# The first FFN's opening down product by seven block products instead of eight

## The chip, the cores and the metric

The kernel runs on one core of a Trainium2 chip. The metric is the device time of one launch in microseconds (us), the median of the runs shown; lower is better. A profiled execution gives the trace, and its own time stands beside those runs.

## The reference, cut to what matters

The kernel computes two layers of an encoder trunk for 640 tokens (512 of a prompt and 8 times 16 of running streams), all in fp32. Each layer has a first FFN, a mixer (convolution and attention) and a second FFN. The change touches the first FFN of the first layer alone, whose definition is:

```python
def _swiglu(h, w_gu, w_down):
    gu = h @ w_gu
    g, u = jnp.split(gu, 2, axis=-1)
    return (jax.nn.silu(g) * u) @ w_down
...
xp = xp + 0.5 * _swiglu(_rmsnorm(xp, norm_ffn1[l]), w_ffn1_gu[l], w_ffn1_down[l])
```

The model width is 1024 (8 tiles of 128), the FFN width 2816 (22 tiles of 128).

## The kernel before, in words

**Operands.** Activations lie with channels on the 128 partitions and the 640 tokens along the free axis, in two halves of 320. Every fp32 operand is split into a high and a low part (`hi` by a cast on ScalarE, called ACT, and `lo = src - hi` on VectorE, called DVE), and a product is three passes on TensorE, called PE: hi by hi, hi by lo, lo by hi. So one 128x128 weight tile against one half of the tokens is 3 matmuls of 320 columns.

**Eight or seven block products.** A plain product multiplies all tiles. A product "by seven" takes a 2x2 block of weights (two rows of tiles, two columns of tiles) and the two token halves with a Strassen-like scheme: seven block products instead of eight, at the price of sums of weights (DVE), sums and differences of activations (DVE) and more intermediate results that are copied out of PSUM (ACT, DVE). The seven are named by their activation operand: X11, X21, XN6, XT5, XT7, X22, XT4. The gate and up products of a tile (`gate_up`, a "unit") are made by seven in every case but four: 84 matmuls a unit, in blocks of 12, in the order X11, X21, XN6, XT5, XT7, X22, XT4.

**The first FFN, "a0".** `FFNS` gives it chunks of 4, 4, 4, 4, 4 and 2 tiles and a plain opening of 4: the gate and up products of tiles 0 to 3 are eight plain products (`opening`, L604), since the operands of the scheme are made meanwhile. Tiles 4 to 21 are units (`gate_up`, L743). The down product of a chunk's tiles is spread over the units of the next chunk. `by_seven` (L78) says for which chunks it is made by seven, by `down_rows` (L936), in two calls of four output rows each (84 matmuls a call), after the second and third unit of the next chunk. For a down product by seven the activations of two neighbouring tiles form a `Pair` (L872): from the even tile's `E` and the odd tile's `O` come X11 and XT5, X21 and X22, and in `rest` XN6, XT7 and XT4; they are split into hi and lo too. In the kernel before, chunk 0 (the opening's tiles) is not by seven: its down product is 8 plain rows of 24 matmuls, two rows after each of the units 4, 5, 6 and 7.

**What sets the order.** The weights come as a stream of 512 KB pieces (`wst`), whose order follows from `ffn_order`; `load` fetches them, `source` makes the sums of weights, `prep` casts a slice (a "slab") of up to 128x1024 to hi, and `flush` queues the subtraction for lo. The hi and lo of slabs have three buffers each. Until unit 6 of this FFN PE, DVE and ACT run in the order in which the program is written (`ORDERED`, L206, and `free`, L1029); from unit 6 on only PE does, and the tile framework orders DVE and ACT. All three take their instructions in order.

Each unit ends with a `tail` (L854) that multiplies the gate by the up result and splits the product; it is put on the list `tails` and called later: in the kernel before at the start of the down rows behind the unit (L1063), in units without such rows ahead in the next unit behind its block X11 (L823), and in `down_rows`. The opening's own splits (`parts`, L688) are put on the same list: unit 4, the first, calls two behind X11 (L774) and the others behind X21 (L788).

In `gate_up` of a later unit the order around the list is:

```python
            mul(pa, s0, 0, X11, every, True, True)
            ACT.copy(c1, pa)
            prep(used[0] + 1)
            ...
            for t in tails:
                t()
            tails.clear()
            ...
            mul(pa, s1, 0, XN6, every, False, True)
            ACT.copy(u2, pa)
            ...
            mul(pa, s2, 0, XT7, every, False, True)
```

XN6, XT7 and XT4 add to one PSUM tile `pa`; what stands in it is copied out between them (`c1`, `u2`), and XT4 waits for DVE's `add(g[:, t2], pa, c5)` behind XT7.

Of the kernel before, what the change touches and what calls it, by code (L numbers as in the profile page):

```python
# [13 lines left out]
ALU = mybir.AluOpType  # L14
# [17 lines left out]
FT = FF // P  # L32
# [36 lines left out]
def chunk_at(name, j):  # L69

    at = 0
    for n in FFNS[name][0]:
        if j < at + n:
            return at, n
        at += n


def by_seven(name, j):  # L78

    at, n = chunk_at(name, j)  # L80
    return n == 4 and at >= FFNS[name][1] and at + n < FT


def ffn_order(name):
# [93 lines left out]
def halves(t):  # L178
    return t.rearrange("p (a b) -> p a b", a=2)
# [3 lines left out]
def trunk(ctx: ExitStack, tc: tile.TileContext, xin, wst, small, pbias, samplebias, kcache, vcache,  # L183
# [36 lines left out]
    def split(hi, lo, src):  # L220
        ACT.copy(hi, src)
        DVE.tensor_tensor(out=lo, in0=src, in1=hi.bitcast(F32), op=ALU.subtract)
# [5 lines left out]
    for kind, inside in kinds():  # L228
        n = len(fourth)
# [371 lines left out]
            ACT.activation(early, epst, AF.Silu)  # L601
            self.known = True

    def opening(fp, name, goff, n, put, tails):  # L604

        ACT.copy(early, epst)
        ex = Expand(fp, name, goff)
        h = []  # L610
        whi, wlo = (wp.tile([P, CH], F32R, tag=f"w{t}", name=f"w{t}0", bufs=3) for t in ("hi", "lo"))
        ready.append((whi, wlo))
        for k in range(KT):
            g = sm[:, goff + k : goff + k + 1]
            hi = hp.tile([P, T], F32R, tag="hhi", name=f"hhi{name}_{k}")
            lo = hp.tile([P, T], F32R, tag="hlo", name=f"hlo{name}_{k}")
            ACT.activation(hi, x[k], AF.Copy, scale=g)
            c = slice(k * P, (k + 2) * P)
            if k % 2 == 0:
                ACT.copy(whi[:, c], raws[0][:, c])  # L620
            DVE.scalar_tensor_tensor(out=lo, in0=x[k], scalar=g, in1=hi.bitcast(F32),
                                     op0=ALU.mult, op1=ALU.subtract)
            if k % 2 == 0:
                DVE.tensor_tensor(out=wlo[:, c], in0=raws[0][:, c], in1=whi[:, c].bitcast(F32),
                                  op=ALU.subtract)
            h.append((hi, lo))
        flush()

        made = {2: (0, 1), 3: (2, 3), 4: (4,), 5: (5, 6), 6: (7,)}
        us, gs, ps = [], [], []  # L630

        def out(i):

            j, up = divmod(i, 2)
            if not up:
                gs.append(tmp(f"g{name}_{j}"))
                if j:
                    scaled(gs[j], ps[i], ex.rho)
                    ACT.activation(gs[j], gs[j], AF.Silu)
                else:  # L640
                    ACT.copy(halves(gs[j]), two(ps[i]))
                return
            u = tmp(f"u{name}_{j}") if j > 1 else fp.tile([P, T], F32, tag="cap", name=f"u{name}_{j}", bufs=5)
            us.append(u)
            if j:
                scaled(u, ps[i], ex.rho)
                DVE.tensor_tensor(out=u, in0=u, in1=gs[j], op=ALU.mult)
            else:
                ACT.copy(halves(u), two(ps[i]))

        def begun():
            ex.total(att(f"nps{name}"))
            ex.root()
            ex.diagonal()

        at = {2: {4: begun}, 3: {1: lambda: ex.spread([att(f"nbc{name}_{a}")[:, :HT] for a in range(2)])}}
        for i in range(2 * n):
            ps.append(acc(f"po{name}_{i}"))
            product(ps[i], h, at.get(i, {}))
            if i > 1:  # L660
                out(i - 1)
            if i == 0:
                for k in range(KT):
                    ex.square(k)
                    ex.add()
                    if k == 1:
                        out(0)
                    if k == 4:
                        flush()
            if i == 1:  # L670
                continue
            if i == 3:
                g, u = gs[0], us[0]
                DVE.tensor_tensor(out=g, in0=g, in1=ex.rho, op=ALU.mult)
                ACT.activation(g, g, AF.Silu)
                DVE.tensor_tensor(out=u, in0=u, in1=ex.rho, op=ALU.mult)
            flush()
            for m in made.get(i, ()):
                ex.final(m, False)
            if i == 3:  # L680
                DVE.tensor_tensor(out=u, in0=u, in1=g, op=ALU.mult)
            if i == max(made):
                ex.rest()
        ahead()
        begin()
        out(2 * n - 1)

        def parts(j, u):  # L688
            hi = hp.tile([P, T], F32R, tag="hhi", name=f"ahi{name}_{j}")
            lo = hp.tile([P, T], F32R, tag="hlo", name=f"alo{name}_{j}")  # L690
            split(hi, lo, u)
            put(j, (hi, lo))


        for j in sorted(range(n), key=lambda j: j < 2):
            tails.append(lambda j=j: parts(j, us[j]))
        ex.rest = None
        return ex

# [40 lines left out]
        with soon():  # L740
            last(pa)

    def gate_up(fp, n, ex, first, tails, put, j, pair, later, at):  # L743

        pa, pb, pc = (att(f"p{i}{n}")[:, :HT] for i in "abc")

# [15 lines left out]
        if first:  # L762
# [24 lines left out]
            add(u[:, t1], pb, c1)  # L787
            for t in tails[2:]:  # L788
                t()
            tails.clear()  # L790
            s2 = quiet()
            prep(len(ready))
            flush()
# [78 lines left out]
    class Pair:  # L872
# [8 lines left out]
        def product(self, n, u, g, hi, lo):  # L881
            if self.E is None:

                z = self.E = self.fp.tile([P, 3, HT], F32, name=f"de{n}", tag="even", bufs=1)
                DVE.tensor_tensor(out=z[:, 0:3:2], in0=halves(u), in1=halves(g), op=ALU.mult)
                DVE.tensor_tensor(out=z[:, 1], in0=z[:, 0], in1=z[:, 2], op=ALU.subtract)
                at, kinds = slice(0, 2), (X11, XT5)
            else:

                z = self.O = self.fp.tile([P, 5, HT], F32, name=f"do{n}", tag="odd", bufs=1)  # L890
                DVE.tensor_tensor(out=z[:, 3:5], in0=halves(u), in1=halves(g), op=ALU.mult)
                at, kinds = slice(3, 5), (X21, X22)
                self.later.append(self)
                self.work = self.rest()
            flush()
            ACT.copy(halves(hi), z[:, at])
            self.low(halves(lo), halves(hi), z[:, at])
            self.keep(kinds, hi, lo)

        def low(self, lo, hi, z):  # L900
            DVE.tensor_tensor(out=lo, in0=z, in1=hi.bitcast(F32), op=ALU.subtract)
# [6 lines left out]
        def rest(self):  # L908
            E, O = self.E, self.O
            for o, a, b in ((XN6, E[:, 1], O[:, 4]), (XT4, O[:, XN6], O[:, 3])):  # L910
                DVE.scalar_tensor_tensor(out=O[:, o], in0=a, scalar=-1.0, in1=b,
                                         op0=ALU.mult, op1=ALU.subtract)
            DVE.tensor_tensor(out=O[:, XT7], in0=O[:, 4], in1=E[:, 2], op=ALU.subtract)
            yield
            hi, lo = (hp.tile([P, T], F32R, tag=f"h{i}", name=f"t{i}{self.name}") for i in ("hi", "lo"))
            ACT.copy(halves(hi), O[:, 1:3])
            yield
            self.low(halves(lo), halves(hi), O[:, 1:3])
            self.keep((XN6, XT7), hi, lo)
            yield  # L920
            hi, lo = (self.fp.tile([P, HT], F32R, tag=f"t4{i}{self.i}", name=f"t4{i}{self.name}", bufs=1)
                      for i in ("hi", "lo"))
            ACT.copy(hi, O[:, 0])
            yield
            self.low(lo, hi, O[:, 0])
            self.keep((XT4,), hi, lo)
            yield
# [90 lines left out]
    def ffn(name, fp, ex, goff, after, end=False):  # L1018
# [7 lines left out]
        hold[0] = True  # L1026

        mode = ExitStack()
        free = min(j for j in range(FT) if by_seven(name, j)) + 2  # L1029

        def order(engines):
            mode.close()
# [1 line left out]

        order(ORDERED)
        if plain:
            ex = opening(fp, name, goff, plain, act.__setitem__, tails)
        for what, a in ffn_order(name):
            if what == "gu" and a == free:
                order({mybir.EngineType.PE})  # L1040
# [4 lines left out]
            if what == "gu":  # L1045
                pair = None
                if by_seven(name, a):
                    i, odd = divmod(a - chunk_at(name, a)[0], 2)
                    if not odd:
                        at = chunk_at(name, a)[0]  # L1050
                        rows = at and by_seven(name, at - 1)
                        pairs[a] = Pair(fp, f"{name}_{a}", i, later, TURNS[i if rows else i + 2])
                    pair = pairs[a - odd]
                gate_up(fp, f"{name}_{a}", ex, a == plain, tails, act.__setitem__, a, pair, later,
                        a - chunk_at(name, a)[0])
                continue
            if what == "rows":
                ms, js = a
# [145 lines left out]
    class Operands:  # L1204
# [24 lines left out]
        def parts(self, hi, lo, z):  # L1229
            ACT.copy(hi, z)  # L1230
            DVE.tensor_tensor(out=lo, in0=z, in1=hi.bitcast(F32), op=ALU.subtract)
# [496 lines left out]
    fp = ExitStack()  # L1728
# [157 lines left out]
```

## Time and profile before

| | |
|---|---|
| median of 3 runs | 2522.48 us (2522.24 to 2522.82) |
| profiled execution | 2522.74 us, its span 2521.0 us |
| granted TensorE clock, mean | 0.999 |
| busy: PE, weight loads | 2502.0 us (99%), 2441.3 us (97%) |
| busy: DVE, ACT, POOL | 2117.7 us (84%), 1325.1 us (53%), 185.6 us (7%) |
| instructions | 42929, of them 17192 matmuls |

A row of the timeline gives start, duration, engine, line and operation, output and input tiles, shape, count and the idle time before it with what ended it. A duration is longer than the step from one instruction to the next on the same engine, since neighbours overlap. In the table of windows each row is a stretch of the span: its length, each engine's busy time with its number of instructions, the granted TensorE clock and the share of the DMA engines.

### The profile page before, as it was taken

The numbers are of one execution on the slowest core, as the hardware profiler recorded it, in microseconds if no ns is written. First come the engines' busy times: TensorE is split into PE (matmuls) and PEld (weight loads), VectorE is DVE, ScalarE is ACT, GpSimd is POOL, SyncE is SP. The second block draws the span as 40 slices with busy tenths as digits, with TensorE's granted clock in tenths as the row PEclk, the third lists the DMA queues.
The fourth block names the chain that finished last, engine by engine and source line by source line (L and its number), as shares of the span: only waits on it lengthen the run. The fifth ranks groups of instructions, "written<-read, shape, count | busy, mean of one in ns | idle before, by whom it ended". The sixth has DMA issues, their size and how long they took to land.

```text
span 2521.0 us, 42929 instructions
## 1 busy us (share of the span) xinstructions
PE 2502.0 (99%) x17192; PEld 2441.3 (97%) x17192; DVE 2117.7 (84%) x3347; ACT 1325.1 (53%) x2084; POOL 185.6 (7%) x249
## 2 busy tenths in 40 slices
PE   9999999999999999999999999999999999999998
PEld 9999999888999999999999999998889999999998
DVE  7889888878677899988699999888786768899997
ACT  7445556664444545555455555557644455455553
POOL 0000112111000001000001000021110000010000
PEclk9999999999999999999999999999999999999999
DMA  4233444334222234343224343443342222243434
GB/s 144 76 105 103 115 115 126 107 114 162 76 85 92 75 101 115 105 110 100 84 76 112 110 116 100 115 118 124 129 138 84 76 93 76 86 114 109 123 100 99
DMA packets 99320, 265.40 MB, mean 105 GB/s; under 512 B 9680, under 2 KB 45136, under 8 KB 99120
## 3 DMA queue, kind: packets, MB, share of 16 engines
q1 hardware_dynamic: 69408, 220.76, 26.7%
q0 software_dynamic: 28992, 41.26, 9.3%
q8 instruction: 135, 2.21, 0.4%
q10 hardware_dynamic: 720, 0.65, 0.1%
q14 instruction: 65, 0.53, 0.1%
HBM read 222.70 MB, written 7.94 MB: 91 GB/s over the span
## 4 chain that ended last, share of the span: by engine, by line
PE 92%; ACT 4%; DVE 3%; issue 1%; DMA 0%; DVEq 0%; ACTq 0%
PE pab L397 12%; PE paa L397 11%; PE pcb L397 6%; PE pca L397 6%; PE daa L952 5%; PE py L374 4%; PE po L374 4%; PE qa L397 4%; PE pdb L374 4%; PE dab L952 4%; PE pbb L397 3%; PE pba L397 3%; PE poa L374 2%; PE pda L374 2%; PE pv L1392 2%; PE ma_cv L397 2%
## 5 line engine op out<-in xcount | busy, mean ns | idle before, releaser
L312 DVE TENSOR_TENSOR wlo<-raw,whi 128x1024 fp32r<-128x1024 f32 (+1 forms) x566 | 585.6, 1037 | 177.8 <-ACT whi L307 172.6
L307 ACT CAST whi<-raw 128x1024 fp32r<-128x1024 f32 (+1 forms) x566 | 509.1, 903 | 366.6 <-PE pbb L397 38.6
L307 ACT CAST whi<-s 128x1024 fp32r<-128x1024 f32 (+1 forms) x152 | 144.4, 950 | 279.5 <-issue 89.3
L397 PE MATMUL pab<-xhib,whi 128*128 128x320 f32 x704 | 218.1, 310 | 0.3
L397 PE MATMUL pab<-xhib,wlo 128*128 128x320 f32 x704 | 217.3, 309 | 0.0
L397 PE MATMUL pab<-xlob,whi 128*128 128x320 f32 x704 | 217.2, 309 | 0.0
L397 PE MATMUL paa<-xhia,whi 128*128 128x320 f32 x640 | 198.0, 309 | 1.0 <-ACT c_a L833 0.6
L397 PE MATMUL paa<-xhia,wlo 128*128 128x320 f32 x640 | 197.5, 309 | 0.0
L397 PE MATMUL paa<-xloa,whi 128*128 128x320 f32 x640 | 197.5, 309 | 0.0
L312 DVE TENSOR_TENSOR wlo<-s,whi 128x1024 fp32r<-128x1024 f32 (+1 forms) x152 | 166.3, 1094 | 9.8 <-ACT whi L307 9.8
L397 PEld LDWEIGHTS pab<-xhib,whi 128*128 128x128 f32 x704 | 132.1, 188 | 0.9 <-ACT c_b L833 0.8
L397 PEld LDWEIGHTS pab<-xlob,whi 128*128 128x128 f32 x704 | 132.1, 188 | 0.2
L397 PEld LDWEIGHTS pab<-xhib,wlo 128*128 128x128 f32 x704 | 132.1, 188 | 0.0
L397 PEld LDWEIGHTS paa<-xhia,whi 128*128 128x128 f32 x640 | 120.1, 188 | 1.6 <-ACT c_a L833 0.9
L397 PEld LDWEIGHTS paa<-xloa,whi 128*128 128x128 f32 x640 | 120.1, 188 | 0.1
L397 PEld LDWEIGHTS paa<-xhia,wlo 128*128 128x128 f32 x640 | 120.1, 188 | 0.0
L976 POOL DMA_DIRECT2D x<-c_b x28 | 33.8, 1209 | 1105.6 <-ACT c_b L969 457.8
L397 PE MATMUL pcb<-xhib,wlo 128*128 128x320 f32 x352 | 108.8, 309 | 0.0
L397 PE MATMUL pcb<-xlob,whi 128*128 128x320 f32 x352 | 108.6, 309 | 0.0
L397 PE MATMUL pcb<-xhib,whi 128*128 128x320 f32 x352 | 108.6, 309 | 0.0
L976 POOL DMA_DIRECT2D x<-c_a x36 | 43.6, 1212 | 865.1 <-ACT whi L307 386.4
L251 DVE TENSOR_TENSOR raw<-raw,raw 128x512 f32<-128x512 f32 x152 | 103.7, 683 | 0.8
(681 smaller groups left out, 7943.2 us busy)
## 6 DMA issues: line engine op xcount, KB each, us to landing
raw<-in_wst SPq DMA_DIRECT2D x378, 512.0 KB, 3.5
x<-c_a POOLq DMA_DIRECT2D x36, 320.0 KB, 4.2
x<-c_b POOLq DMA_DIRECT2D x28, 320.0 KB, 4.1
kc<-in_kcache SPq DMA_DIRECT2D x32, 256.0 KB, 3.8
vc<-in_vcache SPq DMA_DIRECT2D x16, 512.0 KB, 4.7
x<-u_a POOLq DMA_DIRECT2D x18, 320.0 KB, 5.4
x<-u_b POOLq DMA_DIRECT2D x14, 320.0 KB, 5.5
bias<-in_pbias POOLq DMA_DIRECT2D x16, 256.0 KB, 3.6
```

The source lines that it names most:

```text
L251: DVE.tensor_tensor(out=out, in0=a, in1=b, op=ALU.add)
L307: ACT.copy(hi[:, d], src[:, c])
L312: DVE.tensor_tensor(out=lo, in0=src, in1=hi.bitcast(F32), op=ALU.subtract)
L374: PE.matmul(ps[:, a, :HT], w, x[:, a * HT : (a + 1) * HT], start=first and j == 0, stop=last and j == 2)
L397: PE.matmul(ps, a, b, start=start and kp == 0 and j == 0, stop=stop and kp == NP - 1 and j == 2, skip_group_check=True)
L952: PE.matmul(ps[u], w, y, start=start and i == 0 and j == 0, stop=i == 1 and j == 2, skip_group_check=True)
L976: POOL.dma_start(rows(r, cols), z, accum_op=ALU.add)
L1392: PE.matmul(pv[t], xx[:, t * P : (t + 1) * P], w[:, kk * AW : (kk + 1) * AW], start=c == 0 and kk == 0 and j == 0, stop=c == KT // 2 - 1 a ...
```

## The change

`by_seven` now holds for chunk 0 too, so the down product of tiles 0 to 3 is made by two calls of `down_rows`, after units 5 and 6, instead of 8 plain rows after units 4 to 7. The opening's activations become two `Pair`s (0 and 1, 2 and 3). Since the opening has already multiplied gate and up, `Pair.times` copies the product on ACT where there is no gate. Pair 2/3 is made in unit 4 (parts 2 and 3 behind X11, its `rest` in one piece behind X21). Pair 0/1 is kept for unit 5: the list `after` (parts 0 and 1 and their `rest`) becomes the list of tails at the end of unit 4's first half, unit 4's own tail is put behind it, and all four are called behind X11 of unit 5. Two more things follow. Unit 4 has no down rows behind it, so its tail moves into unit 5. And pair 4/5 takes its later steps at the places of `TURNS` for chunks that follow a chunk by seven. `free` stays 6.

```diff
 def by_seven(name, j):
 
     at, n = chunk_at(name, j)
-    return n == 4 and at >= FFNS[name][1] and at + n < FT
+    return n == 4 and at + n < FT
...
-        def parts(j, u):
+        def parts(j):
             hi = hp.tile([P, T], F32R, tag="hhi", name=f"ahi{name}_{j}")
             lo = hp.tile([P, T], F32R, tag="hlo", name=f"alo{name}_{j}")
-            split(hi, lo, u)
+            pairs[j - j % 2].product(f"{name}_{j}", us[j], None, hi, lo)
             put(j, (hi, lo))
 
-
-        for j in sorted(range(n), key=lambda j: j < 2):
-            tails.append(lambda j=j: parts(j, us[j]))
+        for i in range(n // 2):
+            pairs[2 * i] = Pair(fp, f"{name}_{2 * i}", i, later, ())
+
+        def rest(i):
+            for _ in pairs[2 * i].work:
+                pass
+
+        tails += [lambda: parts(2), lambda: parts(3), lambda: rest(1)]
+        after += [lambda: parts(0), lambda: parts(1), lambda: rest(0)]
         ex.rest = None
         return ex
...
             for t in tails[2:]:
                 t()
-            tails.clear()
+            tails[:] = after
             s2 = quiet()
...
                 z = self.E = self.fp.tile([P, 3, HT], F32, name=f"de{n}", tag="even", bufs=1)
-                DVE.tensor_tensor(out=z[:, 0:3:2], in0=halves(u), in1=halves(g), op=ALU.mult)
+                self.times(z[:, 0:3:2], u, g)
                 DVE.tensor_tensor(out=z[:, 1], in0=z[:, 0], in1=z[:, 2], op=ALU.subtract)
...
                 z = self.O = self.fp.tile([P, 5, HT], F32, name=f"do{n}", tag="odd", bufs=1)
-                DVE.tensor_tensor(out=z[:, 3:5], in0=halves(u), in1=halves(g), op=ALU.mult)
+                self.times(z[:, 3:5], u, g)
                 at, kinds = slice(3, 5), (X21, X22)
-                self.later.append(self)
+                if self.spots:
+                    self.later.append(self)
                 self.work = self.rest()
...
+        def times(self, out, u, g):
+            if g is None:
+                ACT.copy(out, halves(u))
+            else:
+                DVE.tensor_tensor(out=out, in0=halves(u), in1=halves(g), op=ALU.mult)
...
-        free = min(j for j in range(FT) if by_seven(name, j)) + 2
+        free = min(j for j in range(plain, FT) if by_seven(name, j)) + 2
```

The other lines of the diff hand the lists and the pairs through (`opening(..., tails, held, pairs, later)`, `gate_up(..., held if plain else ())`).

More of the change, by code (lines that the diff above doesn't have):

```diff
@@ L602, in spread, with opening @@
             self.known = True
-    def opening(fp, name, goff, n, put, tails):
+    def opening(fp, name, goff, n, put, tails, after, pairs, later):
         ACT.copy(early, epst)
@@ L741, in seven, with gate_up @@
             last(pa)
-    def gate_up(fp, n, ex, first, tails, put, j, pair, later, at):
+    def gate_up(fp, n, ex, first, tails, put, j, pair, later, at, after=()):
         pa, pb, pc = (att(f"p{i}{n}")[:, :HT] for i in "abc")
@@ L1036, in ffn @@
         if plain:
-            ex = opening(fp, name, goff, plain, act.__setitem__, tails)
+            held = []
+            ex = opening(fp, name, goff, plain, act.__setitem__, tails, held, pairs, later)
         for what, a in ffn_order(name):
@@ L1054, in ffn @@
                 gate_up(fp, f"{name}_{a}", ex, a == plain, tails, act.__setitem__, a, pair, later,
-                        a - chunk_at(name, a)[0])
+                        a - chunk_at(name, a)[0], held if plain else ())
                 continue
```

## The prediction

> **What bounds the kernel now.** I read the page first, then the windows of the units around the change, then the timelines of PE, DVE and ACT there.
>
> ```profile
> span 2521.0 us, 42929 instructions
> PE 2502.0 (99%) x17192; PEld 2441.3 (97%) x17192; DVE 2117.7 (84%) x3347; ACT 1325.1 (53%) x2084; POOL 185.6 (7%) x249
> ```
>
> PE is busy nearly all the time, so a matmul less is time won, but only where nothing else makes PE wait. DVE at 84% is the next engine.
>
> The windows that I cut at PE's first block of each unit (columns: length, then busy time and instructions of PE, weight loads, DVE, ACT, POOL, then clock and DMA share):
>
> ```profile
> 67.06:86.42 19.36, 19.36 (x134) 19.36 (x133) 17.19 (x25) 9.68 (x14) 0.00 (x0) 1.00 0.25 82
> 86.42:105.79 19.37, 19.37 (x135) 19.37 (x133) 15.19 (x23) 7.31 (x11) 0.00 (x0) 1.00 0.26 82
> ...
> 144.52:156.84 12.32, 12.32 (x86) 12.32 (x85) 9.83 (x17) 5.87 (x9) 0.00 (x0) 1.00 0.27 86
> 156.84:181.48 24.64, 24.64 (x170) 24.64 (x169) 23.45 (x37) 13.64 (x19) 2.96 (x3) 1.00 0.35 97
> 181.48:206.55 25.07, 24.95 (x171) 24.68 (x170) 20.72 (x30) 13.08 (x19) 3.40 (x4) 1.00 0.53 126
> ```
>
> Rows one and two are units 4 and 5, each with two plain down rows behind it; then unit 8 alone, unit 9 with a `down_rows`, unit 10 with the second one. A unit of 84 matmuls takes 12.32 us, so a matmul steps by 0.1467 us and a block of 12 by 1.76. 24.64 is exactly two units' worth: no wait. 25.07 is 0.43 more: the second `down_rows` of a chunk stalls PE a little. DVE is filled to 17.19 of 19.36 in unit 4 and its rows, and to 23.45 of 24.64 where a unit and rows by seven stand together.
>
> **Part one, the matmuls.** Eight plain rows are 8 x 24 = 192 matmuls, two `down_rows` are 168. 24 x 0.1467 = 3.5 us less. That is 0.14%, and about 0.2% (5 us) is what a measurement of this kernel can tell from no change: what decides is the cost on the other engines.
>
> **Part two, where the new work lies.** Units 4 and 5 and the first `down_rows` run DVE and ACT in program order. The prices are the steps from start to start, in unit 4's own rows (ACT first, then DVE):
>
> ```profile
> 68.36 1.06 ACT L307 CAST whi<-raw 128x1024 fp32r<-128x1024 f32 x1 [1.92 <-DVE raw L251]
> 69.31 0.42 ACT L767 COPY c_a<-paa 128x320 f32<-128x320 f32 x1
> 69.62 1.36 ACT L221 CAST ahia<-ua 128x640 fp32r<-128x640 f32 x2
> 70.88 0.43 ACT L777 COPY c_a<-pca 128x320 f32<-128x320 f32 x1
> 72.54 0.42 ACT L786 COPY c_a<-paa 128x320 f32<-128x320 f32 x1 [1.23 <-PE paa L397]
> ...
> 69.85 1.22 DVE L312 TENSOR_TENSOR wlo<-raw,whi 128x1024 fp32r<-128x1024 f32 x1
> ...
> 76.78 0.48 DVE L251 TENSOR_TENSOR ga<-paa,c_a 128x320 f32<-128x320 f32 x1
> ...
> 81.12 0.68 DVE L251 TENSOR_TENSOR s<-raw 128x512 f32<-128x512 f32 x1
> 81.84 0.69 DVE L251 TENSOR_TENSOR s<-s,raw 128x512 f32<-128x512 f32 x1
> 82.45 0.82 DVE L857 TENSOR_TENSOR ga<-ga,rhoa 128x640 f32<-128x640 f32 x1
> 83.30 0.82 DVE L885 TENSOR_TENSOR dea<-ua,ga 128x640 f32<-128x640 f32 x1
> 84.16 0.49 DVE L886 TENSOR_TENSOR dea<-dea 128x320 f32<-128x320 f32 x1
> 84.57 1.22 DVE L312 TENSOR_TENSOR wlo<-s,whi 128x1024 fp32r<-128x1024 f32 x1
> 85.70 0.82 DVE L901 TENSOR_TENSOR aloa<-dea,ahia 128x640 fp32r<-128x640 f32 x1
> 86.44 0.69 DVE L251 TENSOR_TENSOR raw<-raw,raw 128x512 f32<-128x512 f32 x1
> 87.04 0.69 DVE L251 TENSOR_TENSOR raw<-s,raw 128x512 f32<-128x512 f32 x1
> ```
>
> Steps on ACT: 0.96 (1024 wide), 0.63 (640), 0.32 (320); a 512 cast I take half-way, 0.53. On DVE: 1.14 (1024), 0.74 (640), 0.41 (320), 0.60 (512), and 0.12 more where an instruction reads the result of the one just before. A result can be read by another engine about 0.05 after its shown duration. With these I walk the three queues; the same walk of the order before puts unit 5's first block at 86.55, where the trace has 86.42.
>
> *Unit 4.* Unstalled, PE starts its blocks at 67.06, 68.82, 70.58, 72.34, XT7 at 74.10, 75.86, XT4 at 77.62. DVE starts at 69.85 with the slab's lo: 1.14, then pair 2's difference 0.41 (71.40). ACT casts it 71.53 to 72.26; DVE has idled 0.9; low part to 73.05. ACT copies and casts part 3 until 73.67, DVE idles 0.7, low part to 74.46. The copy of `u2` that XT7 needs stands behind these casts and ends at 74.32: XT7 0.3 late. Then DVE: 0.41 for u, the three sums of `rest` 1.36, 0.9 idle for their cast, low parts 0.74 + 0.41, the slab's lo 0.60, and only then the add to g that XT4 needs, done at 79.38. XT4 starts at 79.43 instead of 77.62: **1.8 us** of waiting in unit 4. Before, `rest` was not there, and the same add ran at 76.8.
>
> *Unit 5.* The down rows that stood between units 4 and 5 (48 x 0.1467 = 7.0 us in which DVE caught up) are gone, so unit 5 starts right behind and waits 0.3 for its first lo and 0.2 for its second. DVE is behind. From 79.3 it does 0.54 and 0.41 for unit 4's g and u, 1.14 for unit 5's first lo, 1.34 for the two weight sums of its second slab, 0.41 for g, idles 0.83 for the cast of that slab, then its lo 1.14 and the sums of slab three 1.20: 86.3. Now the four list items come, ahead of all of unit 5's own copies on both queues. ACT: the slab's cast 0.96, copy of part 0; DVE waits for it until 88.19. Then DVE: difference 0.41, the slab's lo 1.14, low 0.74, 0.44 waiting, low 0.74, three sums 1.36, 0.9 waiting, low 0.74 + 0.41, and tail 4: 0.74 + 0.87 + 0.54. That ends at 97.3. Only then can ACT cast tail 4's operand (0.63), and behind it in ACT's queue stands the copy of `u2`, done at 98.41. XT7 was ready at 88.76. **9.7 us** of waiting.
>
> This queue is in the trace already, in the other layer's first FFN, where one tail lies in the same place of its second unit (waits of PE, then ACT's timeline):
>
> ```profile
> PE paa L397 <- ACT c_a L833: 0.6, 1, 0.6
> ...
> 1285.14 0.73 ACT L896 CAST ahia<-dea 128x640 fp32r<-128x640 f32 x1 [0.50 <-DVE dea L886]
> 1285.77 0.42 ACT L833 COPY c_a<-paa 128x320 f32<-128x320 f32 x1
> ```
>
> L833 is the copy of `u2`, L896 the tail's cast that waits for DVE. One item just overruns the block; here there are four.
>
> *The first `down_rows` and unit 6.* Its operands are ready by then. Its evictions are 3.0 us on DVE (three 640, two 320) and some 2 on ACT, its weights three 1024 slabs and a 512, with four 512 sums. Together with tail 5 DVE stays 2 to 3 us behind PE, which costs PE little: 0.6 us until the second `down_rows` (lo of unit 6's second slab late). The second `down_rows` I give the 0.4 that it has elsewhere. Cover goes nowhere else: POOL is at 0.00 in the windows of units 4 and 5, so its six added accumulating transfers queue behind nothing, the weight bytes stay the same, and the DMA share of 0.53 in the last window is far from full.
>
> **Part three, the clock.** A PE that has been idle comes back slow. At the kernel's start matmul pairs step by 0.53, later by 0.29; at the end, where PE is nearly idle, the granted clock falls to half:
>
> ```profile
> 8.25 0.74 PE L374 MATMUL poa<-hloa,whi 128*128 128x320 f32 x2
> 8.78 0.74 PE L374 MATMUL poa<-hhia,wlo 128*128 128x320 f32 x2
> ...
> 12.36 0.46 PE L374 MATMUL poa<-hloa,whi 128*128 128x320 f32 x2
> 12.65 0.46 PE L374 MATMUL poa<-hhia,wlo 128*128 128x320 f32 x2
> ...
> 5.86:11.45 5.59, 5.59 (x21) 5.47 (x21) 5.12 (x9) 4.96 (x8) 0.00 (x0) 1.00 1.02 389
> ...
> 2506.00:2513.40 7.40, 6.06 (x49) 5.68 (x47) 5.40 (x13) 2.80 (x7) 0.00 (x0) 1.00 0.29 102
> 2513.50:2520.00 6.50, 1.22 (x2) 0.50 (x2) 4.49 (x11) 0.00 (x0) 0.00 (x0) 0.50 0.83 284
> ```
>
> The 21 matmuls of the first 5.59 us step by 0.267 instead of 0.147 (the clock column shows 1.00 there, since the record of the clock begins with a change; I go by the steps): 21 x 0.12 = **2.5 us**. A 9.7 us hole should bring this back once; shorter ones need not. Bounds: nothing (the clock holds) and twice that. The Trainium skill, "TensorE: Matmul & The Clock Gate", section "What's actually happening", says that the clock halves after an idle window of about 3.4 us and comes back after a busy one; the rows above agree, and by a 3.4 us warm-up it would cost about 1.5 instead of 2.5.
>
> **Sum.** -3.5 + 1.8 + 0.5 + 9.7 + 0.6 + 0.4 + 2.5 = **+12.0 us**. The profiled execution (2522.74, of which 1.74 lie outside its span) would become 2534.7; it stands 0.26 over the median, so the median goes from 2522.5 to **2534.5**. If DVE's idling in the walk vanished (some 7.3 us with the small waits), XT7 of unit 5 would come 12.0 - 7.3 = 4.7 late in all, the clock would hold, and the change would end near +1. If shown durations counted instead of steps, about 28 instructions of DVE cost 0.08 more each: +14.
>
> **Rivals.** (A) *The matmuls alone count.* PE is the fullest engine, and DVE at 84% and ACT at 53% absorb the rest: 3.5 less and 0.4 for the second rows, 2519.4, no change that a measurement tells. For it: PE never waits in the four units before, and by the windows a unit with rows by seven runs unstalled at 24.64. The Trainium skill, "Perfetto Trace Analysis", section "Identifying the Most-Contended Engine", says to improve the engine with the highest occupancy first; here PE. Against: those units are ordered by the framework, and no opening's pairs are made there. It decides if the copy of `u2` in unit 5 is not behind the casts. 3%. (B) *DVE and ACT overlap better*: the hole is 2 to 5 us, the clock holds, -3.5 + 1.8 + 3.5 + 1 = about +3, 2525.5: within the bound. 6%. (C) *The clock holds although the hole is as walked*: 2532.0. 13%. (D) *DVE does not catch up*: it gains 24.64 - 23.45 = 1.2 per unit and rows, and with 3 us behind at unit 6 it needs more than one such stretch; PE then waits about 3 more in units 6 to 8: 2537.5. 13%.
>
> **How the numbers follow.** The forecast has 64%. With C and D slower has 90%; A and B make 9% within 0.2%; nothing offers 5 us of gain, so 1% is left for faster. The range runs from a hole 4 us shorter without a slow clock, 2528, to D with a little more, 2538.5.
>
> **What would show it.** Right: PE's matmuls fall by 24; a wait of PE on ACT for the copy of `u2` near 8 to 11 us in one piece, about 20 us after unit 4's start; behind it some 20 matmuls at 0.27; a smaller wait of XT4 of unit 4 on DVE; DVE busy without gaps from 70 to about 120. Wrong: PE without waits between 67 and 141, or a copy of `u2` that runs ahead of the tail's cast.

## The result and the profile after

The changed kernel takes 2534.06 us (median of 6 runs, 2533.51 to 2534.72); the kernel before took 2522.82 us beside it (2522.24 to 2523.11). The ratio is 1.0045 with an interval of 1.0035 to 1.0056: 11.2 us slower. The profiled execution took 2533.69 us, with a span of 2531.6.

The head of the page after:

```profile
span 2531.6 us, 42953 instructions
PE 2500.7 (99%) x17168; PEld 2438.6 (96%) x17168; DVE 2131.2 (84%) x3373; ACT 1336.9 (53%) x2104; POOL 192.7 (8%) x255
```

The 24 matmuls are gone (17192 to 17168), DVE has 13.5 us more to do and ACT 11.8, and still the shares of PE, DVE and ACT are the same. From these shares alone one would not see a loss. The waits of PE after, longest first:

```profile
PE paa L397 <- ACT c_a L839: 10.2, 2, 9.6
PE poa L374 <- ACT whi L620: 5.7, 1, 5.7
PE paa L397 <- DVE ga L251: 1.3, 1, 1.3
```

The second row is the start of the kernel and was there before. The first is new, nearly all in one piece, and L839 is the copy of `u2`; the other 0.7 us of that row lies in the other layer's first FFN, where the kernel before waited 0.6, and the rows of this copy in the experiments hold it too. The third is unit 4's XT4 behind the add to g. PE's timeline around the long wait:

```profile
88.34 0.30 PE L397 MATMUL pca<-xhia,wlo 128*128 128x320 f32 x1
98.20 0.63 PE L397 MATMUL paa<-xhia,whi 128*128 128x320 f32 x1 [9.56 <-ACT c_a L839]
98.63 0.47 PE L397 MATMUL paa<-xloa,whi 128*128 128x320 f32 x1
98.90 0.47 PE L397 MATMUL paa<-xhia,wlo 128*128 128x320 f32 x1
...
101.83 0.47 PE L397 MATMUL pca<-xloa,whi 128*128 128x320 f32 x1
102.10 0.35 PE L397 MATMUL pca<-xhia,wlo 128*128 128x320 f32 x1
102.29 0.31 PE L397 MATMUL pca<-xhia,whi 128*128 128x320 f32 x1
102.44 0.31 PE L397 MATMUL pca<-xloa,whi 128*128 128x320 f32 x1
```

The last block before the hole (the long wait of PE) ends at 88.48 (88.34 and one step); XT7 begins at 98.20. Behind it matmuls step by 0.27 until 102.1 and by 0.15 from then on. DVE's timeline at the end of the hole:

```profile
94.86 0.82 DVE L863 TENSOR_TENSOR ga<-ga,rhoa 128x640 f32<-128x640 f32 x1
95.71 0.82 DVE L911 TENSOR_TENSOR dea<-ua,ga 128x640 f32<-128x640 f32 x1
96.57 0.49 DVE L892 TENSOR_TENSOR dea<-dea 128x320 f32<-128x320 f32 x1
```

ACT's timeline in the same stretch shows what held the copy:

```profile
93.95 0.61 ACT L307 CAST whi<-raw 128x512 fp32r<-128x512 f32 x1
97.09 0.73 ACT L903 CAST ahia<-dea 128x640 fp32r<-128x640 f32 x1 [2.53 <-DVE dea L892]
97.73 0.42 ACT L839 COPY c_a<-paa 128x320 f32<-128x320 f32 x1
```

ACT idles 2.5 us with a finished PSUM tile to copy, because the instruction in front of that copy waits for DVE. That is tail 4, the last item of the list, in the order that the prediction walked.

The windows after, cut at the starts of blocks and at the clock's changes (length, busy time of PE, weight loads, DVE, ACT, POOL, clock, DMA share, GB/s):

```profile
79.47:88.48 9.01, 9.01 (x60) 8.78 (x60) 6.41 (x10) 3.67 (x5) 0.00 (x0) 1.00 0.18 60
88.60:98.10 9.50, 0.04 (x1) 0.00 (x0) 8.11 (x13) 4.69 (x9) 0.00 (x0) 0.68 0.17 55
92.00:102.00 10.00, 3.80 (x14) 3.80 (x15) 6.12 (x11) 3.93 (x7) 0.00 (x0) 0.50 0.19 70
98.20:103.61 5.41, 5.41 (x25) 5.41 (x25) 2.58 (x5) 1.22 (x2) 0.00 (x0) 0.63 0.28 97
...
105.37:117.69 12.32, 12.32 (x87) 12.32 (x86) 12.22 (x18) 7.02 (x10) 2.44 (x2) 1.00 0.30 93
117.69:130.34 12.65, 12.58 (x87) 12.32 (x85) 11.56 (x19) 5.91 (x8) 1.37 (x2) 1.00 0.72 156
130.34:143.06 12.72, 12.58 (x87) 12.32 (x86) 11.39 (x17) 8.12 (x12) 2.54 (x3) 1.00 0.41 108
```

In the hole DVE is busy 8.1 of 9.5 us: it is working off the list. The clock stands at half between 92 and 102. The two blocks XT7 and X22 take 5.41 us instead of 3.52, 1.9 more. Then the first `down_rows` runs at 12.32 without a wait (DVE at 12.22 of it), unit 6 is 0.33 and the second `down_rows` 0.40 over.

### The profile page after: what moved, and what is told of

Its sections match the earlier page's. It is cut to its first block, busy times and chain, and to the rows that moved or that the text cites. A ratio compares the mean times of both kernels' runs of the same rounds, so it can differ in the third digit from the quotient of the medians.

```text
span 2531.6 us, 42953 instructions
## 1 busy us (share of the span) xinstructions
PE 2500.7 (99%) x17168; PEld 2438.6 (96%) x17168; DVE 2131.2 (84%) x3373; ACT 1336.9 (53%) x2104; POOL 192.7 (8%) x255
## 4 chain that ended last, share of the span: by engine, by line
PE 88%; DVE 6%; ACT 4%; issue 1%; DMA 0%; SPq 0%; DVEq 0%; ACTq 0%
PE pab L397 12%; PE paa L397 10%; PE pcb L397 6%; PE pca L397 5%; PE daa L965 5%; PE py L374 4%; PE po L374 4%; PE qa L397 4%; PE pdb L374 4%; PE dab L965 4%; PE pbb L397 3%; PE pba L397 2%; PE pv L1406 2%; PE ma_cv L397 2%; PE dca L965 2%; PE ma_qk L397 2%
## 5 line engine op out<-in xcount | busy, mean ns | idle before, releaser
L312 DVE TENSOR_TENSOR wlo<-raw,whi 128x1024 fp32r<-128x1024 f32 (+2 forms) x568 | 586.3, 1035 | 174.8 <-ACT whi L307 170.2
L307 ACT CAST whi<-raw 128x1024 fp32r<-128x1024 f32 (+2 forms) x568 | 510.2, 902 | 357.3 <-PE pbb L397 38.6
L397 PE MATMUL paa<-xhia,whi 128*128 128x320 f32 x640 | 198.9, 311 | 11.9 <-ACT c_a L839 10.2
L312 DVE TENSOR_TENSOR wlo<-s,whi 128x1024 fp32r<-128x1024 f32 (+1 forms) x154 | 168.5, 1094 | 10.6 <-ACT whi L307 10.6
```

The lines of the kernel that those rows point to most:

```text
L307: ACT.copy(hi[:, d], src[:, c])
L397: PE.matmul(ps, a, b, start=start and kp == 0 and j == 0, stop=stop and kp == NP - 1 and j == 2, skip_group_check=True)
```

## The experiments

Two questions were open behind the trace. Is it the order of two in-order queues that makes the hole, or simply that DVE has more work in units 4 to 6 than PE's time holds? And is the slow clock a term of its own? Each kernel ran in five rounds beside the kernel before, which took 2522.71 us in the first four comparisons and 2522.60 in the last two.

### The pairs left out

```diff
         def parts(j):
...
-            pairs[j - j % 2].product(f"{name}_{j}", us[j], None, hi, lo)
+            split(hi, lo, us[j])
             put(j, (hi, lo))
+            p = pairs[j - j % 2]
+            p.keep((X21, X22) if j % 2 else (X11, XT5), hi, lo)
+            if j % 2:
+                p.keep((XN6, XT7), hi, lo)
+                p.keep((XT4,), hi, lo)
...
-        tails += [lambda: parts(2), lambda: parts(3), lambda: rest(1)]
-        after += [lambda: parts(0), lambda: parts(1), lambda: rest(0)]
+        for j in (2, 3, 0, 1):
+            tails.append(lambda j=j: parts(j))
```

> Leaves out the making of the opening's pairs: the four products are split as in the kernel before (behind the same blocks of unit 4), XN6, XT7 and XT4 of chunk 0 use these splits as stand-ins; the two down_rows stay, and unit 4's tail stays in unit 5. Theory P (the pairs' work in units 4 and 5 makes the hole): the hole is gone, -3.5 for the matmuls, about +1.8 in small waits behind unit 4's tail and in unit 6, +0.3 in the second down_rows: 2521.3, 1.5 under the kernel before. Rival S (the lost down rows between units 4 and 5, in which DVE caught up, make the hole with or without pairs): PE still waits over 4 us for the copy of u2 in unit 5, 2526 or more.

Measured: 2521.68 us (2521.11 to 2522.73), ratio 0.9996, interval 0.9987 to 1.0005. Its waits of PE for L844, the copy of `u2` here:

```profile
PE paa L397 <- ACT c_a L844: 1.6, 2, 0.9
```

The hole is gone and what is left is a wait of 0.9 behind tail 4, near the 0.6 that the other layer showed before. So losing the 7 us of down rows does not make the hole by itself; it takes the pairs' work on top. Since parts 0 and 1 are back in unit 4 here, this run does not separate the amount of that work from its place in unit 5; the later runs do. The seven products alone bring about 1 us, not 3.5, and the interval does not exclude no change at all: small waits take the rest, the largest of them behind tail 4 in its new place.

### PE kept busy in the hole

```diff
             spot("e4")
+            if n == "a0_5":
+                fill = acc("fill")
+                for i in range(60):
+                    PE.matmul(fill[:, 0, :HT], s1[0][:, :P], ex.ops[0][0][:, X11],
+                              start=i == 0, stop=i == 59)
             mul(pa, s2, 0, XT7, every, False, True)
```

> The changed kernel, with 60 more matmuls (8.8 us) between XT5 and XT7 of unit 5, into PSUM that nobody reads, so that PE is busy while it waits. If the slow clock behind the hole is a term of its own (1.9 us in the trace of the changed kernel): no half clock near 92 to 102 us, the rest unchanged, 2532.2. Rival (the matmuls behind the hole are slow for another reason, operands that come late for instance): 2534.1 as before the filling, and slow steps still behind XT7.

Measured: 2532.04 us (2531.74 to 2533.05), ratio 1.0037, interval 1.0025 to 1.0050; 2.0 under the changed kernel's 2534.06. The window of the whole stretch has a clock of 1.00, where the changed kernel's stands at 0.50 for 10 us:

```profile
66.00:150.00 84.00, 81.68 (x547) 80.03 (x547) 72.69 (x108) 42.64 (x64) 7.46 (x6) 1.00 0.35 94
```

XT7 and X22 take 3.63 us here (99.39 to 103.02), where they took 5.41. So the clock's price is a term of its own, about 2 us, and the rest of the loss is the waiting.

### Unit 4's tail out of the list

```diff
-            for t in tails:
+            k = 3 if n == "a0_5" else len(tails)
+            for t in tails[:k]:
                 t()
-            tails.clear()
+            del tails[:k]
             spot("e2")
```

> The changed kernel with unit 4's tail (2.2 us of DVE and a cast) taken out of unit 5's list and called in the first down_rows, ahead of unit 5's own tail. Theory Q (one copy stands in a bad place; what is taken from in front of it is won): the hole shrinks by about 4 us, 2530. Theory D (DVE is in debt through units 4 and 5 and rows, in program order; what leaves unit 5 makes PE wait in the down_rows for its own ACT copy): a hole of about 6 in unit 5, a second of 3 to 4 at the down_rows' XT7, a slow clock behind them: 2535 to 2537.

Measured: 2535.27 us (2534.94 to 2536.70), ratio 1.0050, interval 1.0038 to 1.0063. Its waits of PE:

```profile
PE paa L397 <- ACT c_a L840: 6.9, 2, 6.3
PE poa L374 <- ACT whi L620: 5.7, 1, 5.7
PE daa L966 <- ACT u_a L980: 3.5, 1, 3.5
```

The windows behind its two holes, with the clock in the last column but two:

```profile
92.00:98.00 6.00, 3.16 (x12) 3.16 (x13) 3.06 (x6) 3.20 (x6) 0.00 (x0) 0.50 0.22 65
112.00:118.00 6.00, 5.38 (x20) 5.38 (x21) 4.56 (x7) 2.16 (x4) 1.71 (x2) 0.50 0.13 26
```

What leaves unit 5 comes back as a hole of 3.5 in the first `down_rows`, whose own copy (`u2_`, L980) now stands behind tails 4 and 5. On ACT the cast of tail 5 waits for DVE in front of it:

```profile
111.24 0.72 ACT L904 CAST ahia<-doa 128x640 fp32r<-128x640 f32 x1 [3.33 <-DVE doa L912]
111.87 0.70 ACT L980 ACTIVATE u_a<-daa 128x640 f32<-128x640 f32 x1
```

Both holes bring a slow clock: XT7 and X22 take 5.05 us behind the first and 6.26 behind the second, for 3.52 at full speed. Nothing is won. The median is 1.2 us above the changed kernel's, but the two intervals overlap, so it is not shown that two short holes cost more than one long one. As long as the order in the queues stays as it is, moving an item only moves the wait.

### The framework's order from unit 4 on

```diff
-        free = min(j for j in range(plain, FT) if by_seven(name, j)) + 2
+        free = plain or min(j for j in range(plain, FT) if by_seven(name, j)) + 2
```

> The changed kernel with DVE and ACT ordered by the framework from unit 4 on instead of unit 6 (PE in program order as before). Theory O (the program order of the two queues makes the hole; the work itself would fit into PE's time): no hole over 2 us, the clock holds, waits of about 2 to 3 us in all, 2521 to 2523. Rival W (DVE has more work in these units than PE's time holds, whatever the order): holes of 8 us or more in sum remain, 2529 or more.

Measured: 2522.01 us (2521.67 to 2522.84), ratio 0.9997, interval 0.9988 to 1.0006: the same work, the same list, 12 us less than the changed kernel. Its waits of PE:

```profile
PE paa L397 <- DVE ga L251: 0.7, 1, 0.7
...
PE paa L397 <- ACT c_a L839: 0.7, 1, 0.7
...
PE paa L397 <- DVE wlo L312: 0.4, 1, 0.4
```

The first is XT4 of unit 5, the third lies in unit 6. The second is the other layer's: in this FFN PE no longer waits for the copy of `u2`.

ACT's timeline in its unit 5:

```profile
83.13 0.73 ACT L903 CAST ahia<-dea 128x640 fp32r<-128x640 f32 x1
83.76 0.73 ACT L903 CAST ahia<-doa 128x640 fp32r<-128x640 f32 x1
84.39 0.73 ACT L929 CAST thia<-doa 128x640 fp32r<-128x640 f32 x1
85.02 0.62 ACT L307 CAST whi<-raw 128x512 fp32r<-128x512 f32 x1
85.54 0.43 ACT L839 COPY c_a<-paa 128x320 f32<-128x320 f32 x1
86.71 1.05 ACT L307 CAST whi<-raw 128x1024 fp32r<-128x1024 f32 x1 [0.74 <-ACT c_a L839]
87.67 0.45 ACT L936 CAST t4hia<-doa 128x320 fp32r<-128x320 f32 x1
88.03 0.42 ACT L842 COPY c_a<-pca 128x320 f32<-128x320 f32 x1
89.08 0.73 ACT L903 CAST ahia<-dea 128x640 fp32r<-128x640 f32 x1 [0.64 <-DVE dea L892]
```

The three casts of pair 0/1 run back to back, without idle time, and the copy of `u2` follows them: ACT's copies of the two products already ran in unit 4 (75.34 and 76.16), and the differences on DVE that the casts wait for were queued earlier. The cast of tail 4, which held the copy in the changed kernel, now comes 3.5 us behind it (89.08 for 85.54). The framework also starts pair 2/3 before unit 4 (its first copy at 62.14). Which of these moves is worth how much was not separated. The rival that DVE's work does not fit falls. What is left of the waits is DVE's debt: from 79.3 to 91.6, most of unit 5, DVE is never idle and PE waits 0.7.

```profile
79.30:91.60 12.30, 11.58 (x77) 11.10 (x77) 12.30 (x21) 7.30 (x13) 0.00 (x0) 1.00 0.18 71
```

### The tails deferred, in both orders

The edit on top of the last one puts tail 4 into the first `down_rows`, tail 5 into unit 6, and pair 4's sums behind unit 6's XN6. The second kernel has the same places without the change of `free`.

```diff
+            k = 3 if n == "a0_5" else len(tails)
+            for t in tails[:k]:
                 t()
+            del tails[:k]
...
+            k = 1 if n == "a0_0_0" else len(tails)
+            for t in tails[:k]:
                 t(False)
+            del tails[:k]
...
+                        if (name, a) == ("a0", 4):
+                            spots = ("g2e3",) + spots[1:]
```

> As e4_pe_only (the framework orders DVE and ACT from unit 4 on), and the two tails are deferred: unit 4's is called in the first down_rows, unit 5's in unit 6, and pair 4's first sums behind unit 6's XN6. Theory O with debt (what e4 still waits, about 2 us in units 5 and 6, is DVE's debt, and the tails aren't needed before the next chunk's down_rows): the waits of units 5 and 6 go, about 0.3 is left in unit 4 and 0.4 in the second down_rows, 2520.0, so 2.7 under the kernel before and near the 3.5 of the matmuls. Rival (the debt only moves on to units 6 and 7): 2522.

Measured: 2520.18 us (2519.59 to 2522.23), ratio 0.9991, interval 0.9982 to 1.0000. The engines' line of its page:

```profile
PE 2498.8 (99%) x17168; PEld 2437.5 (97%) x17168; DVE 2129.5 (85%) x3373; ACT 1337.3 (53%) x2104; POOL 192.5 (8%) x255
```

One window over units 4 to 8 and both `down_rows` (and 1 us of unit 9), which PE fills to 88.19 of 88.40:

```profile
67.00:155.40 88.40, 88.19 (x599) 87.55 (x598) 85.58 (x132) 49.01 (x74) 7.41 (x6) 1.00 0.41 106
```

This is 2.4 under the kernel before, with an interval that ends at 1.0000, so it is at the edge of what these runs can tell; the traces agree with it: from unit 4's first matmul to the end of unit 7 it takes 74.79 us (67.33 to 142.12), where the kernel before takes 77.46 (67.06 to 144.52) and the changed kernel 88.23 (67.15 to 155.38). It is 13.9 under the changed kernel, with the same matmuls and the same number of DVE and ACT instructions. DVE is at 85.58 of 88.40, so there is little left to hide more behind.

> The same deferred tails, but DVE and ACT in program order until unit 6 as in the changed kernel. If placing the items is enough: waits under 3 us, 2521 to 2523. If the order in which DVE and ACT alternate inside the list counts (casts that wait for a DVE difference, with the copy of u2 behind them): a hole of 6 to 7 us in unit 5, about 1 in the down_rows and 1 in unit 6 remain, and a short slow clock: 2531 to 2533.

Measured: 2532.78 us (2532.18 to 2533.23), ratio 1.0040, interval 1.0028 to 1.0053. Its waits of PE, and the cast of pair 0/1 that stands in front of the copy on ACT:

```profile
PE paa L397 <- ACT c_a L840: 7.0, 2, 6.3
...
93.15 0.72 ACT L930 CAST thia<-doa 128x640 fp32r<-128x640 f32 x1 [2.22 <-DVE doa L927]
```

The places alone do not help: a hole of 6.3 stays while DVE and ACT alternate in program order. The order takes the loss away (2522.01); the deferred tails bring 1.8 more on top of it (2520.18) and little without it (2532.78 for 2534.06).

## Why the prediction was right

It said 2534.5, slower, in 2528 to 2538.5; 2534.06 was measured. The terms, the trace after taken between the same blocks:

| term | predicted | trace after |
|---|---|---|
| 24 matmuls | -3.5 | -3.5 |
| unit 4, XT4 behind `rest` on DVE | +1.8 | +1.8 (79.47 for 77.71) |
| unit 5's first two slabs | +0.5 | +0.2 |
| unit 5, XT7 behind the list | +9.7 | +9.7 (98.20 for 88.48) |
| half clock behind the hole | +2.5 | +1.9 |
| unit 6 | +0.6 | +0.3 |
| second `down_rows` | +0.4 | +0.4 |
| sum | +12.0 | +10.8 |

The span grew by 10.6. The walk of the three queues carried the two large terms to within 0.1 us, since steps of ACT and DVE hardly vary from one place of this kernel to another: tail 4 takes DVE 2.20 us in the rows above (94.86 to 97.06), 2.15 in the walk. Both ends of the long wait came 0.2 to 0.3 us before the walk's (88.48 for 88.76, 98.20 for 98.46), so their difference fits better than either. Three smaller terms were too large: the waits for slabs whose lo came just late, unit 6, and the clock. The clock's term took the kernel's start as its measure, where 21 matmuls were slow; here it was 15 (98.20 to 102.1). It has no fixed price in these runs: over XT7 and X22 it cost 1.9 here, 1.5 and 2.7 behind the two holes of the kernel with tail 4 moved, and 2.6 in the last kernel of the experiments (95.13 to 101.23, 6.10 for 3.52). That 2.5 came as near as it did is luck in part. The profiled executions differ by 10.95 (2533.69 for 2522.74): 10.6 in the span, and 0.35 around it (2.09 for 1.74), which no term had. The median missed by only 0.4, and that too is partly luck: the terms were 1.2 too large in sum, and the 0.35 and a kernel before that ran 0.34 slower beside the changed one (2522.82 for 2522.48) made up for most of it.

The row of the other layer, one tail in the same place with a wait of 0.6, was the right witness: the same copy, the same cast in front. Rival A, the matmuls alone, failed on the point that it named, the copy behind the casts, and rival B, a hole of 2 to 5 us, on the hole of 9.7. Rival D, a debt that PE goes on paying, cost 0.3 in unit 6. Rival C, a clock that holds, was measured by filling the hole: 2532.04, where it said 2532.0. One sign failed: DVE was to be busy without gaps from 70 to about 120, and it idles 1.79 us for a copy of ACT before 88.10 and 2.79 for PE before 101.87. The walk itself had DVE idling some 7 us, so the sign did not follow from it.

The Trainium skill, "TensorE: Matmul & The Clock Gate", section "What's actually happening", puts both turns of the clock at about 3.4 us of idling or work. Here PE's last block ended at 88.48 and the clock was at half in the window from 92, and 3.9 us after XT7's start the steps were short again: this trace agrees roughly, and its price was 1.9, between the 1.5 by that page and the 2.5 taken from the kernel's start. The other traces scatter around that figure. In windows of 0.1 us the clock falls 2.8 and 2.7 us after PE's last block in the kernel with tail 4 moved and 5.2 after it in the last kernel, and comes back 3.2, 5.8 and 5.5 us after PE's next start; the kernel's start had slow steps for 5.6 us.

## What to carry to other kernels

A saving on the fullest engine is worth only what the in-order queues beside it let through: look for the copies out of PSUM that PE waits for, and count what stands in front of them in their queue and what that in turn waits for on the third engine. If the new work fits into the engines' time, as 85.58 of 88.40 did here, change the order in which two engines alternate before giving up the saving; moving an item from one place of the same order to another only moved the wait. A walk of the queues with start-to-start steps from the trace, tried first on the order that is there, sized this hole to a few tenths of a microsecond; a slow clock behind a hole is better given as a range (1.5 to 2.7 us here).

## What was not expected of the hardware

Already a hole of some 3.7 us (3.5 of it idle) halved the clock: behind the second hole of the kernel with tail 4 moved the window from 112 to 118 shows 0.50. A longer hole did not cost more clock. In windows of 0.1 us the clock stands at half for 6.8 us in each of the holes of 3.7, 6.5 and 6.5 us (both of the kernel with tail 4 moved, then that of the last kernel) and for 10.2 in the one of 9.7. What a hole costs beyond its own length is the part of that stretch that falls behind it: 5.8 us after the shortest, where XT7 and X22 lost 2.7, and 3.9 after the longest, where they lost 1.9. The hole of some 1.4 us in unit 4 (1.3 of it idle) cost nothing but itself, with the clock at 1.00 in the window from 79.47 to 88.48.
